# The first mixer's first 1024 columns, multiplied in step with the modulation

## The chip, the cores and the metric

The kernel runs on one core of a Trainium2 chip. The metric is the device time of one execution in microseconds (us), with the weights and inputs in HBM. The core's engines are TensorE (PE, its weight loads PEld), VectorE (DVE), ScalarE (ACT), GpSimd (POOL) and SyncE (SP), which issues nearly all loads.

## The reference

256 tokens of 1024 channels pass through three blocks, in float32. Only the start matters here:

```python
cond = silu(c)
mod = cond @ ada_w[layer] + ada_b[layer]          # 6 x 1024 values for each of 2 layers
shift1, scale1, gate1, shift2, scale2, gate2 = split(mod, 6)
hn = rmsnorm(x, norm1_w) * (1 + scale1) + shift1
# first mixer (mLSTM)
proj = hn @ w_in                                  # 3088 columns
qk = silu(causal_conv(proj[:, :1024], conv_w, conv_b))   # q: 512, k: 512
v, o, gates = proj[:, 1024:2048], proj[:, 2048:3072], proj[:, 3072:]
x = x + gate1 * (mixer(q, k, v, gates, o) @ w_out)
hn = rmsnorm(x, norm2_w) * (1 + scale2) + shift2
x = x + gate2 * swiglu(hn)
```

A second layer (a gated linear recurrence and a mixture of 8 experts) and a block with three kinds of attention and a feed-forward follow. They are the same in both kernels.

## The kernel before, in words

The activations lie transposed: 8 chunks of 128 channels on the partitions, 256 tokens along the free dimension. A weight matrix is read in tiles of 1 MiB, [128, 4, 512] (512 rows of 512 columns), by a generator, `all_weights`, that names them in the order of use. `weights()` hands out the next tile and prepares those after it, two ahead (`depth`). Most tiles are split by ScalarE and VectorE into a high and a low part in a shorter format (`whi`, `wlo`), and each product is then three products; tiles whose number stands in `WHOLE` are multiplied unsplit in float32, where each product shows as two records in the trace.

A load goes into a buffer `raw` (4 slots) or `raw2` (2 slots) and is issued on SP's queue when a slot is free. The first three tiles, columns 0 to 511 and half of 512 to 1023, are whole.

The modulation is done on VectorE. `ada_tile` (L478 to L492) loads 256 columns of `ada_w`, 1 MiB, and multiplies each of two blocks of 128 columns with `cond`, adding up along the row. There are 48 such tiles, 24 for each layer, numbered from 0 here. Tiles 0 to 3 give shift1 and 4 to 7 scale1; 8 to 11 give gate1, 12 to 15 shift2, 16 to 19 scale2. After the first norm a tile is done now and then between products: `ada_step(f)` adds up fractions and does one tile for each whole one. In the mixer that is one tile for each tile of weights (`between=step`), in the output's product 0.7 for each of the two tiles that have a `between`. `ada_until(20)` (in `run`) does what is left up to tile 19 before the next norm. These tiles take the `raw2` slots.

Before the first norm, x is squared by chunk on ScalarE. GpSimd adds up the squares of the first six chunks (`together=6`), TensorE then sums them and the last two over the partitions, a chain of small steps on VectorE makes r = 1 / root mean square from it, and TensorE spreads r over the partitions.

`first_norm` does tiles 0, 4, 1, 5, 2, 6, 3, 7 of the modulation; after each pair two chunks of the gain are known. From the second pair on it scales the chunks (VectorE) and adds the shift (ScalarE, into `full`, named `so` in the trace); at the end it splits `full` into act_hi and act_lo. Then `mlstm` multiplies: `convolved(0, q)` the first 512 columns, the two gates' rows (`small`), the chain for the decays, `convolved(1, k)` the next 512 columns with a modulation tile for each of its two weight tiles, then v (`proj_tok`) and the rest. A product of 512 columns holds two of the four accumulator banks `acc`.

The order on each engine is not the program's: a planner goes through the program with its own costs and gives each engine the instruction that comes first in the program among those that it takes for ready; a load is ready when its slot is free. The engines then run their lists in order. `behind(ins)` puts instructions after `ins` on the same engine. `hold` is a list of such instructions for the splits and modulation tiles to come. After the output's product it is set for two of them:

```python
self.hold = [[self.last_resid]] * 2
self.ada_until(20)
```

so the next two modulation tiles come after the last residual on VectorE. The norm that follows needs all of tiles 16 to 19, since `gain(0, 4, ...)` is one instruction over its 8 columns.

## Time and profile before

| what | value |
|---|---|
| time, median of 3 runs | 1485.22 us (1483.94 to 1486.9) |
| profiled execution, first to last instruction (span) | 1481.2 us |
| TensorE busy | 96% of the span, mean granted clock 0.977 |
| VectorE busy | 76% |
| ScalarE busy | 57% |
| transfers | 231 GB/s read over the span |

The profile gives the profiled execution's time as its span; the runs' time holds start and end as well. Busy times are sums of an engine's instructions; on TensorE products overlap, so its busy time is not work at its peak. In the timeline a row is a start, a duration, an engine, a line of the kernel, an operation, output <- inputs, and in brackets the idle time before it and what ended it. A line can be that of a helper: L165 is every product, L175 every step of ScalarE, L178 and L181 most of VectorE, L485 the modulation's products, L194 and L481 the loads of weights and of modulation.

### The profile page before, as it was taken

The numbers are of one execution on the slowest core, as the hardware profiler recorded it, in microseconds if no ns is written. First come the engines' busy times: TensorE is split into PE (matmuls) and PEld (weight loads), VectorE is DVE, ScalarE is ACT, GpSimd is POOL, SyncE is SP. The second block draws the span as 40 slices with busy tenths as digits, with TensorE's granted clock in tenths as the row PEclk, the third lists the DMA queues.
The fourth block names the chain that finished last, engine by engine and source line by source line (L and its number), as shares of the span: only waits on it lengthen the run. The fifth ranks groups of instructions, "written<-read, shape, count | busy, mean of one in ns | idle before, by whom it ended". The sixth has DMA issues, their size and how long they took to land.

```text
span 1481.2 us, 23294 instructions
## 1 busy us (share of the span) xinstructions
PE 1429.3 (96%) x9380; PEld 1292.7 (87%) x9380; DVE 1123.6 (76%) x1738; ACT 838.1 (57%) x1195; POOL 32.9 (2%) x36
## 2 busy tenths in 40 slices
PE   5999899999999998999999999999999999999998
PEld 4789899999999987888888888888878779999998
DVE  6887798887697786897898888888666566765554
ACT  2644444434775655777777777766545355544432
POOL 1000100001000020000000000000000000100000
PEclk7999999999899998999999999999999999999999
DMA  8975599989453334798998998995435234555542
GB/s 335 339 260 195 178 348 353 343 314 337 150 151 109 115 114 145 252 375 309 320 362 305 345 339 303 355 322 192 143 114 169 88 114 143 164 179 191 179 143 86
DMA packets 149508, 343.51 MB, mean 232 GB/s; under 512 B 5904, under 2 KB 27280, under 8 KB 149136
## 3 DMA queue, kind: packets, MB, share of 16 engines
q1 hardware_dynamic: 148240, 341.00, 66.1%
q8 instruction: 76, 1.25, 0.4%
q10 hardware_dynamic: 1152, 0.94, 0.2%
q14 instruction: 40, 0.33, 0.1%
HBM read 340.86 MB, written 1.05 MB: 231 GB/s over the span
## 4 chain that ended last, share of the span: by engine, by line
PE 58%; ACT 1%; DVE 1%; issue 0%; ACTq 0%
PE acc L165 38%; PE ps L165 18%; PE ps L1203 1%; ACT whi L175 1%; PE ps L1290 1%; PE ps L698 0%; DVE wlo L181 0%; ACT L175 0%; PE ps L1413 0%; DVE yel L178 0%; ACT yeh L175 0%; ACT e L175 0%; ACT sg L175 0%; DVE ss L677 0%; DVE e L185 0%
## 5 line engine op out<-in xcount | busy, mean ns | idle before, releaser
L181 DVE TENSOR_TENSOR wlo<-raw,whi 128x1024 fp32r<-128x1024 f32 (+2 forms) x564 | 646.9, 1182 | 148.2 <-ACT whi L175 147.6
L175 ACT ACTIVATE whi<-raw 128x1024 fp32r<-128x1024 f32 (+2 forms) x564 | 547.8, 1016 | 314.1 <-PE acc L165 164.3
L165 PE MATMUL acc<-act_hi,whi 128*128 128x256 f32 x1344 | 382.0, 285 | 2.6 <-ACT act_hi L175 2.4
L165 PE MATMUL acc<-act_lo,whi 128*128 128x256 f32 x1344 | 381.1, 284 | 0.0
L165 PE MATMUL acc<-act_hi,wlo 128*128 128x256 f32 x1344 | 379.6, 283 | 1.3 <-DVE wlo L181 1.3
L165 PEld LDWEIGHTS acc<-act_hi,whi 128*128 128x128 f32 x1344 | 255.2, 190 | 4.7 <-ACT act_hi L175 3.0
L165 PEld LDWEIGHTS acc<-act_hi,wlo 128*128 128x128 f32 x1344 | 255.5, 190 | 1.8 <-DVE wlo L181 1.5
L165 PEld LDWEIGHTS acc<-act_lo,whi 128*128 128x128 f32 x1344 | 255.8, 190 | 0.7
L165 PE MATMUL acc<-whi,act_hi 128*128 128x512 f32 (+1 forms) x560 | 217.5, 388 | 0.1
L165 PE MATMUL acc<-wlo,act_hi 128*128 128x512 f32 (+1 forms) x560 | 216.7, 387 | 0.0
L165 PE MATMUL acc<-whi,act_lo 128*128 128x512 f32 (+1 forms) x560 | 215.6, 385 | 0.0
L165 PEld LDWEIGHTS acc<-whi,act_hi 128*128 128x128 f32 x560 | 105.9, 189 | 20.3 <-issue 0.9
L165 PEld LDWEIGHTS acc<-wlo,act_hi 128*128 128x128 f32 x560 | 105.8, 189 | 20.2 <-issue 1.2
L165 PEld LDWEIGHTS acc<-whi,act_lo 128*128 128x128 f32 x560 | 105.7, 189 | 18.8 <-issue 0.3
L485 DVE SCALAR_TENSOR_TENSOR raw<-raw,cond 128x1024 f32<-128x1024 f32 x96 | 115.3, 1228 | 6.5 <-DMA raw<-in_ada_w_dram 6.5
L165 PE MATMUL ps<-hh,whi 128*128 128x256 f32 x352 | 99.6, 283 | 1.5 <-DVE x L178 1.5
L165 PE MATMUL ps<-hl,whi 128*128 128x256 f32 x352 | 99.5, 283 | 0.0
L165 PE MATMUL ps<-hh,wlo 128*128 128x256 f32 x352 | 99.4, 283 | 0.0
L165 PE MATMUL ps<-wlo,hth 128*128 128x512 f32 x176 | 69.0, 392 | 0.0
L165 PEld LDWEIGHTS ps<-hh,whi 128*128 128x128 f32 x352 | 67.4, 192 | 1.7 <-DVE x L178 1.7
L165 PE MATMUL ps<-whi,htl 128*128 128x512 f32 x176 | 68.8, 391 | 0.0
L165 PE MATMUL ps<-whi,hth 128*128 128x512 f32 x176 | 67.6, 393 | 0.0
(348 smaller groups left out, 1798.2 us busy)
## 6 DMA issues: line engine op xcount, KB each, us to landing
raw<-in_ada_w_dram SPq DMA_DIRECT2D x48, 1024.0 KB, 6.2
raw<-in_moe_w_down_dram SPq DMA_DIRECT2D x40, 1024.0 KB, 6.0
raw<-in_moe_w_up_dram SPq DMA_DIRECT2D x32, 1024.0 KB, 7.3
raw<-in_moe_w_gate_dram SPq DMA_DIRECT2D x32, 1024.0 KB, 7.1
raw<-in_w_in_dram SPq DMA_DIRECT2D x26, 1024.0 KB, 5.2
raw<-in_h_w_in_dram SPq DMA_DIRECT2D x16, 1024.0 KB, 5.8
raw<-in_m_w_in_dram SPq DMA_DIRECT2D x12, 1024.0 KB, 7.3
raw<-in_moe_w_gate_dram SPq DMA_DIRECT2D x16, 768.0 KB, 5.5
```

Source lines behind the costliest of these rows:

```text
L165: self.nc.tensor.matmul(out, l, r, start=start, stop=True, skip_group_check=True)
L175: return self.nc.scalar.activation(out, in_, f, **k)
L181: return self.nc.vector.tensor_tensor(out, a, b, op=op)
L485: last = self.nc.vector.scalar_tensor_tensor(w[:, i, :], in0=w[:, i, :], scalar=1.0, in1=self.cond, op0=ALU.mult, op1=ALU.mult, accum_out= ...
L1203: nc.tensor.transpose(hps[:, f * P : (f + 1) * P], h[:, f * P : (f + 1) * P], self.cst("ident"))
L1290: nc.tensor.transpose(pt[:, j * P : (j + 1) * P], e[:, j * P : (j + 1) * P], self.cst("ident"))
```

## The change

The four first weight tiles are cut the other way, 256 rows (two chunks) by 1024 columns, and all four are whole (`WHOLE` gets 3). `first_norm` does a round for each pair of modulation tiles: both tiles, the load of the weight tile that belongs to these two chunks (into `raw2`), gain, scale and shift of the two chunks, their split, and their products with all 1024 columns, into all four `acc` banks. `mlstm` gets these banks and convolves q and k from them, one after the other and before the gates' rows; the two modulation tiles that were done between k's products are no longer there. All modulation tiles of the first norm use `raw`. x is loaded in two halves, named before `conditions`, and its squares are no longer added up by GpSimd (`together=1`): TensorE sums each chunk. The chain of r is no longer put behind the modulation's products. Docstrings are taken out, which is left out here.

```diff
-WHOLE = {0, 1, 2, 12}
+WHOLE = {0, 1, 2, 3, 12}
...
-        yield from columns("m_w_in", *range(0, 3072, 512))
+        wv = a["m_w_in"].rearrange("(k p) n -> p k n", p=P)
+        yield from [wv[:, k : k + 2, 0:D] for k in range(0, DC, 2)]
+        yield from columns("m_w_in", *range(D, 3072, 512))
...
     def first_norm(self, x):
         act = self.act_tiles()
         g = self.t(self.cp, [P, 8], "gain01")
         shift = self.mod_part(0, 0)
+        banks = [self.bank("acc").rearrange("p (a s) -> p a s", a=2) for _ in range(4)]
         r = None
-
-        def normed(chunks):
-            for c in chunks:
+        for j in range(4):
+            self.ada_tile(0, j, "raw")
+            self.ada_tile(0, 4 + j, "raw")
+            self.tiles += 1
+            self.loaded.append(self.raw(next(self.plan), "raw2"))
+            sl = slice(2 * j, 2 * j + 2)
+            self.stt(g[:, sl], self.mod_part(0, 1)[:, sl], 1.0, self.vec("n1", 2 * j, 2), ALU.add, ALU.mult)
+            if j == 0:
+                r = self.stat_end()
+            for c in range(2 * j, 2 * j + 2):
                 t = self.t(self.tp, [P, S], "sq", 4)
                 self.stt(t, x[:, c, :], g[:, c : c + 1], r, ALU.mult, ALU.mult)
                 self.act(self.full[:, c, :], t, AF.Identity, bias=shift[:, c : c + 1])
-
-        for j in range(4):
-            self.ada_tile(0, j, "raw2" if j % 2 else "raw")
-            last = self.ada_tile(0, 4 + j, "raw")
-            sl = slice(2 * j, 2 * j + 2)
-            self.stt(g[:, sl], self.mod_part(0, 1)[:, sl], 1.0, self.vec("n1", 2 * j, 2), ALU.add, ALU.mult)
-            if j == 0:
-                with self.behind(last):
-                    r = self.stat_end()
-            if j == 1:
-                self.load()
-                normed(range(4))
-            if j > 1:
-                normed(range(2 * j, 2 * j + 2))
-        with self.behind(last):
-            for c in range(0, DC, 2):
-                last = self.split(*[t[:, c : c + 2, :] for t in act], self.full[:, c : c + 2, :])
+            last = self.split(*[t[:, sl, :] for t in act], self.full[:, sl, :])
+            (w,) = self.weights(False)
+            order = [(k, cb) for k in range(2) for cb in range(DC)]
+            if j == 3:
+                order.sort(key=lambda x: x[1])
+            for k, cb in order:
+                self.mm(banks[cb // 2][:, cb % 2, :], w[:, k, cb * P : (cb + 1) * P], self.full[:, 2 * j + k, :], j + k == 0 and cb % 2 == 0)
         self.last_normed = [i.ins for i in last]
+        self.prepare(self.depth)
         self.ada_owed, self.ada_now = 0.0, 8
-        return act
+        return act, banks
...
         with tc.tile_pool(name="cond", bufs=1) as pool:
+            for c in range(0, DC, 4):
+                nc.sync.dma_start(x[:, c : c + 4, :], a["xT"].rearrange("p (c s) -> p c s", c=DC)[:, c : c + 4, :])
             self.conditions(pool)
-            nc.sync.dma_start(x, a["xT"].rearrange("p (c s) -> p c s", c=DC))
-            self.stat_begin()
+            self.stat_begin(together=1)
...
-                act = self.first_norm(x)
-                act = self.mlstm(mlstm, act)
+                act = self.mlstm(mlstm, *self.first_norm(x))
...
-    def mlstm(self, pool, act):
+    def mlstm(self, pool, act, banks):
...
-            for b, bank in enumerate(self.proj_t(act, between=step if g else None)):
+            for b, bank in enumerate(banks[2 * g : 2 * g + 2]):
...
         convolved(0, q)
+        convolved(1, k)
         gp = self.bank()
...
-        convolved(1, k)
         for g in range(2):
```

## Rows read from the trace of the kernel before

**Rows 1.** The page, part 1: busy us, share of the span, instructions of TensorE.
```profile
PE 1429.3 (96%) x9380; PEld 1292.7 (87%) x9380; DVE 1123.6 (76%) x1738; ACT 838.1 (57%) x1195; POOL 32.9 (2%) x36
```

**Rows 2.** Windows: stretch, length, busy us per engine, granted clock, DMA share, GB/s.
```profile
20.00:24.00 4.00, 1.22 (x4) 0.93 (x4) 3.97 (x12) 0.00 (x0) 0.00 (x0) 0.50 1.02 408
...
28.00:32.00 4.00, 4.00 (x13) 3.21 (x13) 3.78 (x10) 0.00 (x0) 0.00 (x0) 0.65 0.99 355
32.00:36.00 4.00, 4.00 (x20) 3.02 (x19) 3.96 (x8) 1.54 (x3) 0.00 (x0) 1.00 0.32 122
72.00:78.40 6.40, 6.40 (x15) 4.31 (x15) 5.12 (x12) 4.46 (x8) 0.00 (x0) 0.50 0.38 119
```

**Rows 3.** Timeline of PE, first 61 us: start us, duration us, operation, count, idle before.
```profile
3.90 3.48 PE L165 MATMUL ps<-cst_base,vecs 128*128 128x128 f32 x16 [3.90 <-DMA cst_base<-in_cst_base_dram]
15.42 2.72 PE L165 MATMUL ps<-cst_base,sq 128*128 128x1 f32 x12 [8.04 <-POOL sq L410]
22.21 1.22 PE L165 MATMUL ps<-cst_base,st1y 128*128 128x128 f32 x4 [4.07 <-DVE st1y L178]
25.44 9.82 PE L165 MATMUL acc<-so,raw 128*128 128x256 f32 x32 [2.00 <-ACT so L175]
35.19 2.78 PE L165 MATMUL ps<-so,gate_w 128*40 128x256 f32 x12
...
40.21 6.31 PE L165 MATMUL acc<-so,raw 128*128 128x256 f32 x28 [1.18 <-ACT so L175]
46.45 1.06 PE L165 MATMUL ps<-so,gate_w 128*40 128x256 f32 x4
47.44 7.17 PE L165 MATMUL acc<-so,raw 128*128 128x256 f32 x32
54.26 0.47 PE L165 MATMUL acc<-act_hi,whi 128*128 128x256 f32 x1
...
60.08 0.40 PE L165 MATMUL acc<-whi,act_hi 128*128 128x512 f32 x1
```

**Rows 4.** Timeline of DVE, first 42 us.
```profile
10.16 1.23 DVE L485 SCALAR_TENSOR_TENSOR raw<-raw,cond 128x1024 f32<-128x1024 f32 x1 [5.98 <-DMA raw<-in_ada_w_dram]
...
18.18 0.16 DVE L187 TENSOR_SCALAR st1v<-ps 128x2 f32<-128x2 f32 x1 [1.72 <-PE ps L165]
...
19.24 1.22 DVE L485 SCALAR_TENSOR_TENSOR raw<-raw,cond 128x1024 f32<-128x1024 f32 x1
...
24.36 0.48 DVE L178 SCALAR_TENSOR_TENSOR sq<-x,gain,ps 128x256 f32<-128x256 f32 x1
...
39.14 0.86 DVE L178 SCALAR_TENSOR_TENSOR sq<-x,gain,ps 128x256 f32<-128x256 f32 x2
```

**Rows 5.** Lines of DVE, 40 to 60 us: count, busy us, mean ns, idle before.
```profile
L178 DVE SCALAR_TENSOR_TENSOR conv<-acc,vecs,conv 128x253 f32<-128x253 f32 (+2 forms) x12 | 5.3, 474 | 1.9 <-ACT conv L175 1.8
```

**Rows 6.** Timeline of all engines, end of the first mixer, 166 to 174 us.
```profile
166.34 0.86 DVE L178 SCALAR_TENSOR_TENSOR x<-acc,mod,x 128x256 f32<-128x256 f32 x2
...
167.12 1.21 DVE L485 SCALAR_TENSOR_TENSOR raw<-raw,cond 128x1024 f32<-128x1024 f32 x1
...
167.37 1.05 PE L165 MATMUL ps<-cst_base,sq 128*128 128x1 f32 x8 [1.10 <-ACT sq L175]
...
169.41 0.14 DVE L187 TENSOR_SCALAR st1v<-ps 128x2 f32<-128x2 f32 x1
169.51 0.37 SPq L481 DMA_DIRECT2D raw<-in_ada_w_dram  x1
...
169.71 0.17 DVE L178 SCALAR_TENSOR_TENSOR gain<-mod,vecs 128x8 f32<-128x8 f32 x1
...
171.17 0.16 DVE L178 SCALAR_TENSOR_TENSOR st1y<-st1h,st1y 128x2 f32<-128x2 f32 x1
...
172.73 1.26 DVE L178 SCALAR_TENSOR_TENSOR sq<-x,gain,ps 128x256 f32<-128x256 f32 x3 [1.40 <-PE ps L165]
```

**Rows 7.** DMA issues in 169 to 170 us: KB, us from issue to landing.
```profile
raw<-in_ada_w_dram SPq DMA_DIRECT2D x1, 1024.0 KB, 5.0
```

## The prediction

> **What bounds the kernel now.** I read the page's busy shares first. TensorE is busy for 96% of the span [rows 1], so what matters is what moves the start of its work, or opens a hole in it. Next came the windows of the first 100 us and then the timeline of each engine there, since the change is a change of the first mixer's start, and last the seam where its output meets the next norm.
>
> In the timeline TensorE's first large product starts at 25.44, and from 40.21 on it has no gap until the v products start at 60.08 [rows 3]. It runs on from there (busy for all of 6.40 us in the window at 72 us [rows 2], even at half clock), so whatever moves 60.08 moves what follows. What sets 25.44 is the factor r of the norm: its sums wait for GpSimd until 15.42 [rows 3], VectorE's chain for it runs from 18.18 with modulation products between its steps, and the first scaled chunk starts at 24.36 [rows 4], 1.08 us before the product. Transfers run at 408 GB/s meanwhile [rows 2], which is 2.6 us for a tile of 1.05 MB.
>
> The seam is the other place. After the last residual (166.34 + 0.86) VectorE does one modulation tile from 167.12 on, because `hold` puts it behind that residual; gain waits for it at 169.71, the chain of r ends at 171.33, and the next norm starts at 172.73 [rows 6]. TensorE has only small products there. So a microsecond added at this seam is a microsecond of the end.
>
> **The change part by part.** The modulation's tiles are numbered from 0.
>
> *When r is ready.* The six squares that GpSimd added up now go to TensorE one chunk at a time: 8 chunks, 32 records instead of 12. They cost 1.05/8 = 0.13 us each at full clock [rows 6] and 2.72/12 = 0.227 at half [rows 3], so 4.2 to 7.3 us, from the end of the spread of c (3.90 + 3.48 = 7.4) to between 11.6 and 14.7. The chain of r takes 171.33 - 169.41 = 1.9 us when nothing is put between its steps [rows 6], its spread 1.22 [rows 3]. The modulation tile 0 lands as before at 10.16 [rows 4] (x was ahead of it and still is), tile 4 2.6 us later; two products of 1.23 each bring VectorE to 15.2, and the small additions of tile 4 to about 15.5. Lower bound: r is done by then and the first product starts 1.08 later, at 16.6. Upper bound: the products of tile 1 stand inside the chain, as at 19.24 [rows 4]. Tile 1 now lands behind a weight tile, at 12.7 + 2 x 2.6 = 17.9, and from 17.9 the rest of the chain as before (19.24 to 25.44) gives 24.1. If VectorE runs the chain after tile 4 and before tile 1, it is 15.2 + 1.9 + 1.2 + 1.1 = 19.4. I take 19.5, because the gap between 15.2 and 17.9 in which tile 1 is not there is as long as the chain: 25.44 - 19.5 = **5.9 us earlier**, with 1.3 and 8.8 as ends.
>
> *TensorE's work from there to the v products.* Before, it is 60.08 - 25.44 = 34.6 us. Now there are four whole tiles of 32 records and 16 records for the gates: 9.82 for the first, which begins at half clock in either kernel (0.50 at 20 to 24 us, the 1.2 GHz level, after small products; 0.65 at 28 to 32, then 1.00 [rows 2]), 3 x 7.17, and 2.78 + 1.06 [rows 3], together 35.2. The whole fourth tile costs 7.17 where the split one took 60.08 - 54.26 = 5.8, and the wait of 1.18 before 40.21 goes. So **0.5 us later**. If the 32 sums keep the clock at full until the first tile, some of its records save half: 9.82 against 7.17 for a tile at full clock, 2.65 us; in the trace the clock is at half after 12 such sums, so I take none of it.
>
> *New waits.* The weights' tiles now take the two `raw2` slots, so the third's load waits until TensorE is through with the first, and the fourth's with the second. Landing goes in steps of 2.6 us from 10.16 on: tiles 0 and 4, a weight tile, 1, 5, a weight tile, 2, 6. Then 3 and 7, whose slots are free by 23, land at 30.8 and 33.4. The third weight tile, asked for at 19.5 + 9.8 = 29.3, comes behind them at 36.0; TensorE wants it at 36.5. A tile of v ahead of it makes it 2.1 late, two 4.7. The fourth, asked for at 36.5, lands 5.0 us later on idle queues [rows 7], 41.5, and is wanted at 43.7: one tile ahead costs 0.4, two 3.0. SP's queue is in order, so behind such a waiting load stand the modulation's last tiles and v's, and VectorE and ScalarE's splits wait for those. I take **0.5 us**, with 0 and 7.7 as ends. The modulation is not late: even behind the third weight tile, 7 lands at 36, and its norm (2.4 + 1.4 us of VectorE and ScalarE) is done by 40. The window at 32 us shows transfers at 0.32 now [rows 2], so there is room for the weights that come sooner.
>
> *Convolutions.* All four accumulators are held by the first product, so v's first two wait for the convolutions of four column blocks: 12 steps of VectorE at 0.474 [rows 5], 5.7 us. They start 1.8 us into the last tile, which is sorted by columns, and end at 43.7 + 1.8 + 5.7 = 51.2, before TensorE has done the last tile and the gates' products (54.7). Hidden; were the gates' products done earlier, v would start up to 3.8 us sooner, not later. The 7.2 us of VectorE's work that leave this stretch (a split of 2.4 and two modulation tiles of 2.4 each) are worth nothing there, since TensorE has the shorter end.
>
> First mixer: -5.9 + 0.5 + 0.5 = **-4.9 us**.
>
> *The seam.* The k columns' product was also the place where two modulation tiles were done (`between=step`, one for each tile of weights). Now 8 + 4 + 4 + 1 = 17 tiles are done when `ada_until(20)` comes, not 19. Three are left: 17, 18, 19. The first two are held behind the last residual; the third takes the slot of the first. It can be asked for only when VectorE is through with tile 17, at 169.5, where the trace issues the next tile now [rows 6], and lands 5.0 us later [rows 7], at 174.5. Its products take 2 x 1.2, additions and gain 0.5: 177.4, where the norm starts at 172.73 now [rows 6]. Tile 18 (2.4 us) and the chain of r (1.9 us, and 1.4 to its spread's end) fit in between, 169.5 to 175.2. That is **+4.7 us**, with 4.2 (a load half a microsecond quicker) and 8 (the chain put behind tile 19) as ends.
>
> By the Trainium skill, page "DMA: Bandwidth & Descriptors", section "Anatomy of one DMA", a transfer costs about 2.0 us and its bytes at 436 GB/s, here an estimate of 4.4 us, on another path than SP's; the row has 5.0. By the rule the seam would cost 4.1 and the sum would be 0.6 us lower; I stay with the row. The same page's "Rules for kernel authors" say to issue a transfer early and wait late, and tile 19 is issued after the point that it holds up: that speaks against this change, and the 5.0 us stand for it.
>
> Sum: -4.9 + 4.7 = **-0.2 us**. The profiled span is 1481.2, the median of the runs 1485.22; the 4.0 us around the span belong to start and end and stay. Forecast: 1485.0.
>
> **Rivals.**
> (a) *Faster.* The sums run at full clock and r is there when tile 4 is: the first product starts at 16.6 to 17.5, 8 to 8.8 us earlier, and the clock may save 2.6. Against it: the sums must run in half the time that the row at half clock has, and the third tile of weights then waits for its load (wanted at 33.6, landing 34 to 36), which takes back up to 2. -8 + 0.5 + 1 + 4.7 = -1.8 without the clock, -4.4 with it: 1481 to 1483. A stretch at clock 0.50 around 72 to 78 us [rows 2], after the many products of 8 rows, makes 6.4 us of what takes 3.2 at full; it may go with the new order, which would give about as much.
> (b) *Slower: the loads behind TensorE.* SP's queue puts the tiles of v or the modulation ahead of the third and fourth weight tile. It decides from two tiles ahead on: 4.7 for the third, 5 us with what the fourth adds, in place of my 0.5: -5.9 + 0.5 + 5 + 4.7 = +4.3, 1489.5. For it speaks that v's loads need only free slots; against it that they come later in the program.
> (c) *Slower: r behind tile 19 at the seam.* If VectorE's order puts the chain of r behind tile 19's products, its 1.9 and the spread's 1.4 come on top: +3.1, 1488.3. It decides where the plan takes the load for quicker than tile 18 and the chain, 4.3 us; now the chain stands behind the one held tile [rows 6].
> (d) *It doesn't do what it says.* The chain of r takes tile 1 and tile 5 into it as now, the first product starts at 24.1 and the stages follow the modulation no closer: -1.3 + 1.0 + 4.7 = +4.4, 1489.6.
>
> **How the numbers follow.** The forecast's case gets 0.50; (a) 0.25, (b) 0.10, (c) 0.07, (d) 0.08. A difference under 0.2%, 3.0 us, can't be told from none here. Of the forecast's case 0.40 lies within that, 0.07 below and 0.03 above; of (a) 0.15 lies below (the part with the clock) and 0.10 within; of (b), (c) and (d) 0.24 lie above and 0.01 within. That makes 0.22 faster, 0.51 the same, 0.27 slower. The range runs from 1479.8 (most of (a)) to 1490.5 (most of (b) to (d)); the likeliest case's own is 1482 to 1488.
>
> **What would show it.** Right: the first large product at 18 to 21 us; no wait over 1 us before the four tiles' products; v's products from 54 to 56; at the seam an issue of a modulation tile right after the first of two held ones, VectorE waiting some 2 us for it, and 4 to 5 us more between the last residual and the norm. Wrong: v's products before 52 or after 59, TensorE waiting for `raw`, tile 19 loaded before the last residual, or a seam no longer than before, which would make the change faster by 5 us.

## The result, and the profile after

The changed kernel takes 1493.61 us (median of 6 runs) where the kernel before takes 1484.58 beside it: 0.56% slower, ratio 1.0056, 95% interval [1.0037, 1.0074]. A second set of 6 runs gave 1490.56 against 1484.72, 1.0046 [1.0030, 1.0062]. So it costs 6 to 9 us; 1485.0 was forecast, and both medians lie above the range. The profiled execution is the fastest of its set (1486.21, span 1484.4). Its busy shares say nothing, as [rows 1] didn't:

```profile
PE 1432.0 (96%) x9384; PEld 1295.1 (87%) x9384; DVE 1120.3 (75%) x1736; ACT 832.6 (56%) x1191; POOL 26.9 (2%) x31
```

The timeline of TensorE in the first 58 us answers [rows 3] (start, duration, operation, count, idle before; in this kernel the modulation's products are at L487 and its loads at L483):

```profile
8.78 4.39 PE L165 MATMUL ps<-cst_base,sq 128*128 128x1 f32 x32 [0.99 <-ACT sq L175]
17.37 1.22 PE L165 MATMUL ps<-cst_base,st1y 128*128 128x128 f32 x4 [4.20 <-DVE st1y L178]
19.78 9.89 PE L165 MATMUL acc<-so,raw 128*128 128x256 f32 x32 [1.19 <-ACT so L175]
29.59 1.06 PE L165 MATMUL ps<-so,gate_w 128*40 128x256 f32 x4
30.58 7.17 PE L165 MATMUL acc<-so,raw 128*128 128x256 f32 x32
...
46.77 7.17 PE L165 MATMUL acc<-so,raw 128*128 128x256 f32 x32
53.87 1.06 PE L165 MATMUL ps<-so,gate_w 128*40 128x256 f32 x4
57.89 0.48 PE L165 MATMUL acc<-whi,act_hi 128*128 128x512 f32 x1 [2.96 <-DVE conv L178]
```

The first product comes at 19.78, 5.7 earlier than in [rows 3], and the tiles follow one another without a wait. But v starts at 57.89, only 2.2 earlier: TensorE waits 2.96 us for VectorE's convolution. VectorE there (beside [rows 5]):

```profile
44.87 0.69 DVE L181 TENSOR_TENSOR act_lo<-so,act_hi 128x512 fp32r<-128x512 f32 x1 [1.24 <-ACT act_hi L175]
49.83 1.00 DVE L178 SCALAR_TENSOR_TENSOR conv<-acc,vecs,conv 128x253 f32<-128x253 f32 x2 [4.27 <-ACT conv L175]
50.77 2.36 DVE L181 TENSOR_TENSOR wlo<-raw,whi 128x1024 fp32r<-128x1024 f32 x2
53.05 0.48 DVE L178 SCALAR_TENSOR_TENSOR conv<-acc,vecs,conv 128x255 f32<-128x255 f32 x1
53.44 2.35 DVE L181 TENSOR_TENSOR wlo<-raw,whi 128x1024 fp32r<-128x1024 f32 x2
55.71 2.42 DVE L178 SCALAR_TENSOR_TENSOR conv<-acc,vecs,conv 128x253 f32<-128x253 f32 x6
```

It idles 4.27 us, and then the splits of v's first two tiles, 4.7 us, stand between the steps of the convolution that frees v's banks; v starts behind the eighth of the nine steps shown, when the first bank is free. ScalarE's half of these splits stands between its own parts of the convolution:

```profile
49.70 3.88 ACT L175 ACTIVATE whi<-raw 128x1024 fp32r<-128x1024 f32 x4
...
53.94 1.00 ACT L175 ACTIVATE conv<-acc,vecs 128x256 f32<-128x256 f32 x2
```

The splits are late because SP asks for v's tiles behind the fourth tile, whose slot is free only at 37.8 (SP's queue; the last of these rows is the fourth tile and three of v):

```profile
29.70 0.37 SPq L194 DMA_DIRECT2D raw<-in_m_w_in_dram  x1
30.16 1.03 SPq L483 DMA_DIRECT2D raw<-in_ada_w_dram  x2
37.79 2.47 SPq L194 DMA_DIRECT2D raw<-in_m_w_in_dram  x4
```

The seam, all engines, beside [rows 6]:

```profile
164.32 0.86 DVE L178 SCALAR_TENSOR_TENSOR x<-acc,mod,x 128x256 f32<-128x256 f32 x2
...
165.11 1.21 DVE L487 SCALAR_TENSOR_TENSOR raw<-raw,cond 128x1024 f32<-128x1024 f32 x1
...
167.50 7.85 SPq L483 DMA_DIRECT2D raw<-in_ada_w_dram  x3
...
169.75 0.15 DVE L187 TENSOR_SCALAR st1v<-ps 128x2 f32<-128x2 f32 x1
...
172.57 1.23 DVE L487 SCALAR_TENSOR_TENSOR raw<-raw,cond 128x1024 f32<-128x1024 f32 x1 [0.89 <-DMA raw<-in_ada_w_dram]
...
175.18 0.17 DVE L178 SCALAR_TENSOR_TENSOR gain<-mod,vecs 128x8 f32<-128x8 f32 x1
```

VectorE does tile 17, tile 18 and the chain of r, waits 0.89 for tile 19, and comes to gain at 175.18 (before 169.71) and to the norm at 175.49 (before 172.73): 4.8 us longer from the last residual.

### Taking the half clock out

Two executions of one program differ by stretches in which TensorE is at a granted clock of 0.50, the 1.2 GHz level. Windows of the two profiles of the kernel before, the first and then the second, which has it for longer:

```profile
72.00:76.00 4.00, 4.00 (x9) 2.49 (x9) 2.72 (x6) 2.79 (x7) 0.00 (x0) 0.50 0.33 121
76.00:80.00 4.00, 4.00 (x13) 3.15 (x13) 4.00 (x9) 1.67 (x2) 0.00 (x0) 0.67 0.70 232
```
```profile
68.00:72.00 4.00, 4.00 (x8) 1.95 (x7) 2.24 (x8) 3.94 (x7) 0.00 (x0) 0.50 1.05 395
72.00:76.00 4.00, 4.00 (x8) 1.78 (x7) 1.31 (x4) 1.04 (x2) 0.00 (x0) 0.50 0.37 135
76.00:80.00 4.00, 4.00 (x9) 2.59 (x9) 2.87 (x7) 2.67 (x5) 0.00 (x0) 0.50 0.00 0
80.00:84.00 4.00, 4.00 (x15) 2.96 (x14) 4.00 (x10) 1.64 (x3) 0.00 (x0) 0.81 0.79 261
```

To compare, I sum busy PE time times (1 - clock) over windows of 4 us from 36 to 160 us and subtract it (at 0.50, half of a window's busy time is taken off). In the table, "first product" and "v" are the starts of the first large product and of the first v product on TensorE, "last residual" is the start of its last instruction, and the seam runs from there to the first instruction of the next norm. (The expectations of a5, b2 and c3 count the seam from the start of the last pair of residuals, 0.4 more; those of a2 and a3 from that pair's end, 0.5 less.) "Half" is the sum, and the ratio is to runs of the kernel before on the same chip. All times in us.

| kernel | first product | v | last residual | half | without half | seam | ratio [95%] |
|---|---|---|---|---|---|---|---|
| before | 25.4 | 60.1 | 166.7 | 3.4 | **163.3** | 6.0 | |
| a5 before again | 25.6 | 60.4 | 170.0 | 6.8 | **163.1** | 6.0 | |
| changed | 19.8 | 57.9 | 164.7 | 1.7 | **163.0** | 10.8 | 1.0056 [1.0037, 1.0074] |
| a1 changed again | 19.8 | 57.8 | 167.8 | 4.9 | **162.8** | 10.6 | 1.0046 [1.0030, 1.0062] |
| a2 tiles into v | 20.3 | 58.2 | 172.9 | 6.0 | 166.9 | 6.1 | 1.0042 [1.0028, 1.0056] |
| a3 before, 3 at seam | 25.7 | 60.4 | 165.7 | 1.7 | 164.0 | 10.8 | 1.0043 [1.0026, 1.0059] |
| a4 v's loads first | 22.3 | 62.9 | 169.5 | 3.2 | 166.4 | 10.7 | 1.0044 [1.0026, 1.0061] |
| c1 convolution whole | 19.7 | 56.7 | 163.3 | 0.0 | 163.3 | 10.8 | 1.0035 [1.0019, 1.0050] |
| b2 tiles into output | 22.3 | 59.3 | 174.0 | 6.8 | 167.2 | 6.1 | 1.0050 [1.0034, 1.0066] |
| c3 c1 and b2 | 22.4 | 59.1 | 170.6 | 3.4 | 167.2 | 6.1 | 1.0025 [1.0011, 1.0040] |
| d1 tiles into the gap | 19.6 | 66.9 | 173.6 | 6.9 | 166.8 | 6.0 | 1.0055 [1.0034, 1.0077] |
| d2 c1 and d1 | 20.1 | 62.8 | 174.0 | 8.1 | 166.0 | 6.1 | 1.0026 [1.0012, 1.0040] |
| d3 tile 19 early | 22.4 | 59.7 | 169.5 | 5.1 | 164.4 | 10.8 | 1.0054 [1.0038, 1.0070] |
| e1 changed less 2 tiles | 19.6 | 57.8 | 164.9 | 1.7 | 163.1 | 6.1 | 1.0003 [0.9989, 1.0018] |
| e2 before less 2 tiles | 25.5 | 60.2 | 166.9 | 3.4 | 163.5 | 6.0 | 0.9995 [0.9980, 1.0010] |
| e3 before, sums alone | 22.5 | 57.2 | 162.2 | 1.7 | **160.4** | 6.0 | 0.9984 [0.9969, 0.9999] |
| e4 c1 less 11 tiles | 22.2 | 58.7 | 169.1 | 6.8 | 162.3 | 6.1 | 1.0004 [0.9988, 1.0020] |
| f1 e3 again | 22.4 | 57.2 | 162.1 | 1.7 | **160.4** | 6.0 | 0.9974 [0.9961, 0.9986] |
| f2 sums and pairs | 20.1 | 62.3 | 167.3 | 4.6 | 162.7 | 6.0 | 1.0012 [0.9997, 1.0026] |

Without the half clock the two profiles of before agree to 0.2 us, those of the changed kernel too, and between the kernels the last residual differs by 0.3 us. The first mixer's gain is gone; the seam's 4.7 is there.

### The profile page after: what moved, and what is told of

Its sections match the earlier page's. It is cut to its first block, busy times and chain, and to the rows that moved or that the text cites. A ratio compares the mean times of both kernels' runs of the same rounds, so it can differ in the third digit from the quotient of the medians.

```text
span 1484.4 us, 23298 instructions
## 1 busy us (share of the span) xinstructions
PE 1432.0 (96%) x9384; PEld 1295.1 (87%) x9384; DVE 1120.3 (75%) x1736; ACT 832.6 (56%) x1191; POOL 26.9 (2%) x31
## 3 DMA queue, kind: packets, MB, share of 16 engines
HBM read 340.86 MB, written 1.05 MB: 230 GB/s over the span
## 4 chain that ended last, share of the span: by engine, by line
PE 58%; ACT 1%; DVE 1%; issue 0%; ACTq 0%
PE acc L165 38%; PE ps L165 18%; PE ps L1205 1%; ACT whi L175 1%; PE ps L1292 1%; PE ps L700 0%; DVE wlo L181 0%; ACT L175 0%; PE ps L1415 0%; DVE yel L178 0%; ACT yeh L175 0%; ACT e L175 0%; ACT sg L175 0%; DVE ss L679 0%; DVE e L185 0%
## 5 line engine op out<-in xcount | busy, mean ns | idle before, releaser
L165 PE MATMUL acc<-act_hi,whi 128*128 128x256 f32 x1328 | 378.2, 286 | 5.0 <-ACT act_hi L175 4.7
L487 DVE SCALAR_TENSOR_TENSOR raw<-raw,cond 128x1024 f32<-128x1024 f32 x96 | 114.3, 1219 | 7.0 <-ACT sq L175 6.1
```

The lines of the kernel that those rows point to most:

```text
L165: self.nc.tensor.matmul(out, l, r, start=start, stop=True, skip_group_check=True)
L487: last = self.nc.vector.scalar_tensor_tensor(w[:, i, :], in0=w[:, i, :], scalar=1.0, in1=self.cond, op0=ALU.mult, op1=ALU.mult, accum_out= ...
```

## The experiments

In the expectations T (later T2, T3) is the account held at that point and R (R1, R2) its rival; a run is then said to bear out one of them, or neither.

**a1, a5: each kernel once more.**

> The changed kernel once more, unaltered, for a second profile. Its first profiled execution has a span only 3.2 us over the one of before, its other executions some 8 to 9. T (the seam's 4.7 us are the loss, the front gives 2.2 back, the rest is small and spread): a profile with a span of 1484 to 1488, the v products again at 57.9, the seam again 4.8 longer. R1 (there is a further loss of 4 to 5 us that the first profile happened not to have): a span of 1489 to 1493, and a stretch in which the two profiles of one program drift apart by that much; if the v products start at 60 or later it sits in the front (a load that lands late), if only the stretch from the third tile of weights on moves, in the loads; if it lies behind 1000 us, in the experts.

> The kernel before once more, unaltered, for a second profile: what two executions of one program differ by. T (the stretches of TensorE at half clock come and go from one execution to the next, 1.6 to 3.4 us each): the same start of the v products at 60.1 and the same seam of 6.4 us, and differences of 1 to 4 us only where a stretch at half clock is there in one and not in the other. R (they are fixed by the program): the two profiles agree to 0.5 us everywhere.

The spans were 1488.5 and 1486.7, against 1484.4 and 1481.2. The starts of v are the same to 0.4 us. The repeat of the changed kernel is longer at half clock, first right after the idle 2.96 us before v (windows of the first profile, then of the repeat):

```profile
59.00:63.00 4.00, 4.00 (x19) 3.23 (x18) 3.97 (x9) 1.60 (x6) 0.00 (x0) 1.00 1.05 395
```
```profile
59.00:63.00 4.00, 4.00 (x13) 3.10 (x12) 3.97 (x9) 1.60 (x6) 0.00 (x0) 0.57 1.04 395
```

13 records where there were 19. The span of a1 lies between T's and R1's; what drifts apart is the time at half clock, as a5's T has it, and no load.

**a3: the seam's change alone, on the kernel before.**

```diff
-            for b, bank in enumerate(self.proj_t(act, between=step if g else None)):
+            for b, bank in enumerate(self.proj_t(act)):
```

> The kernel before, with one edit: the k columns' product does no modulation tiles, so three are left for the seam, as in the changed kernel; the front is otherwise as before. T: the seam from the last residual to the next norm grows from 5.5 to 10.3 us and the time by 4 to 5 us, to 1488.5 to 1490; the v products start up to 1 us earlier, as VectorE has 4.8 us less to do there, so the whole may be 3.5 to 5. R1 (the loss is in the front, in the order of the loads): within 1.5 us of the kernel before. R2 (the change's whole loss of 8 to 9 us comes from leaving three tiles): 8 us slower, 1492 or more.

1490.47, 1.0043: as much as the changed kernel (1.0046, on the same chip), and the seam is 10.8. The time is a little above T's range, and v isn't earlier (60.4), though VectorE has less to do there. So the two tiles that leave the k columns' product are enough for the whole of the loss.

**e1, e2: the same two tiles left out, of the changed kernel and of the one before.** Tiles 18 and 19, or 8 and 9, get the bias alone:

```diff
+        if layer == 0 and j in (18, 19):
+            o = 2 * j
+            with self.held():
+                return self.nc.vector.tensor_copy(self.mod[:, o : o + 2], self.vec("ada_b", o, 2)).ins
```

> The changed kernel without the products and loads of modulation tiles 18 and 19 (their columns get the bias alone): one tile is left at the seam, as in the kernel before. What is left of the change is the front. As I predicted it (front -4.9): 1480 to 1481 against 1485 of the kernel before. T2 (the front gives nothing that lasts): seam 6.0, the last residual at 163 with the half clock taken out, the time 4 to 5.5 us under the changed kernel's and within 1.5 us of the kernel before's, 1484.5 to 1487.

> The kernel before without the products and loads of modulation tiles 8 and 9, the two that stand in the k columns' product (their columns get the bias alone). T2 (they have a free place there): the v products and the last residual within 1 us, the time within 1.5 us of the kernel before's, 1483.5 to 1486. R (they are on the path there too, as anywhere): 3 to 5 us faster, 1480 to 1482, and then the changed kernel only moves what was paid already.

1.0003 and 0.9995: both T2. The two tiles cost nothing in the k columns' product and everything at the seam, and the rest of the change, all of its front, is worth nothing that can be measured (e1's interval runs from 1.6 us faster to 2.7 slower): not the 4.9 us that I forecast.

**d3: is it the late load?**

```diff
-                self.hold = [[self.last_resid]] * 2
-                self.ada_until(20)
+                self.hold = [[self.last_resid]] * 3
+                self.ada_until(19)
+                self.ada_tile(0, 19, "raw")
+                self.ada_now = 20
```

> The changed kernel, but the last of the three modulation tiles at the seam is loaded into a buffer of its own, so that its load doesn't wait for tile 17. As I predicted it, the seam's 4.7 us come from that late load: without it the seam would be 7 to 8.5 us (one more tile of 2.4 on the old 6.0) and the time 2.5 to 4 us below the changed kernel's. T2: the late load hides behind tile 18 and the chain of r, what costs is VectorE's time for two more tiles; the three tiles then run on end, 7.1 us, and the chain and its spread, 3.4, come behind them: a seam of 10.5 to 11.2 and the same time within 1.5 us.

1.0054, and VectorE at the seam:

```profile
169.12 0.86 DVE L178 SCALAR_TENSOR_TENSOR x<-acc,mod,x 128x256 f32<-128x256 f32 x2
...
175.77 1.21 DVE L487 SCALAR_TENSOR_TENSOR raw<-raw,cond 128x1024 f32<-128x1024 f32 x1
...
176.91 0.15 DVE L187 TENSOR_SCALAR st1v<-ps 128x2 f32<-128x2 f32 x1
...
180.29 1.26 DVE L178 SCALAR_TENSOR_TENSOR sq<-x,gain,ps 128x256 f32<-128x256 f32 x3 [1.46 <-PE ps L165]
```

No wait for a load is left, the chain of r now comes behind the third tile, and the seam is 10.8 all the same: T2. VectorE has 4.8 us more to do either way. In the changed kernel the load shows for 0.89, but the wait for the spread of r (1.40 in [rows 6], 1.46 here) is hidden in return, behind tile 19. Three tiles with the load in time and the chain of r ahead of the third could save at most that 0.89; this order wasn't run. My forecast had the seam's size right and its cause too narrow.

**a2, b2: the two tiles elsewhere.** `self.ada_step(f * 1.5)` in v's product (for `f * 1`), or in the output's (for `f * 0.7`).

> The changed kernel, but the v columns' product does 1.5 modulation tiles for each tile of weights instead of 1, so two more tiles are done there and one is left for the seam, as before the change. T (the seam loses 4.7 us because tile 19's load is asked for only after tile 17): the distance from the last residual to the next norm falls from 10.3 to 5.5 us, and the time by 4 to 5 us against the changed kernel, to 1487 to 1490 by its median; against the kernel before it is then between 2 us faster and 4 slower. R (the seam's wait is hidden by what comes later, or VectorE has no room for two more tiles in the v products): the seam is shorter but the time within 1.5 us of the changed kernel's, 1492 to 1495.

> The changed kernel, but the output product of the first mixer does 1.5 modulation tiles for each tile of weights in place of 0.7, so that three come there and one is left for the seam, as before the change. The run with 1.5 in the v products showed the seam back at 6.4 us and the 5 us lost again ahead of it, where VectorE sets the pace. T: in the output product VectorE waits for TensorE for some 3 us twice, so two more tiles of 2.4 us fit; the last residual moves by 0 to 2.4 us, the seam is 6.4 instead of 11.1, and the time falls by 2.5 to 4.7 us, to 1486 to 1489. R (VectorE has no room for them anywhere after the k columns' product has gone): the last residual moves by 4 us or more, the time within 1 us of the changed kernel's.

The seam is back at 6.1 in both, and both are as slow as the changed kernel: R and R. The last residual comes 4 us later, since TensorE now waits for VectorE's chains ahead of it (a2's longest wait, then b2's two; in b2 v starts 1.4 later too, with the slow sums described at the end):

```profile
142.02 5.18 PE L165 MATMUL ps<-cst_base,r8y 128*128 128x128 f32 x32 [3.25 <-DVE r8y L178]
```
```profile
143.43 3.81 PE L165 MATMUL ps<-cst_base,r8y 128*128 128x128 f32 x32 [2.28 <-DVE r8y L178]
148.88 7.17 PE L165 MATMUL acc<-num,raw 128*128 128x256 f32 x32 [1.64 <-DVE num L181]
```

In b2 the products of a modulation tile stand between the steps of that chain (138.65 and 139.88); the free place in the output's product, which T counted on, was used by only one tile more.

**a4, c1: v earlier.** In a4, v's first two tiles are asked for before the modulation's last pair; in c1 after that pair and before the fourth tile, and what follows the first four blocks' convolution on VectorE stays behind it (c1's edit; `last` is the convolution's last instruction):

```diff
-            self.loaded.append(self.raw(next(self.plan), "raw2"))
+            src = next(self.plan)
+            if j == 3:
+                early = [self.raw(next(self.plan)) for _ in range(2)]
+                self.tiles += 2
+            self.loaded.append(self.raw(src, "raw2"))
...
+        self.loaded.extend(early)
...
-        convolved(0, q)
+            return last.ins
+
+        hold = self.behind(convolved(0, q))
+        hold.__enter__()
...
+        hold.__exit__(None, None, None)
```

> The changed kernel, but the first two tiles of v's weights are asked for before the modulation's last pair (tiles 3 and 7) and the fourth tile of the first weights, not behind them. T (the v products start at 57.9 and not at 55 because their tiles land behind the fourth, so that VectorE's splits of them stand between the steps of the convolution that frees the banks): the splits are done before the last tile's products end, the convolution runs unbroken from 49.8, and the v products start at 55.5 to 56.5, 1.5 to 2.4 us earlier, if the modulation's tiles 3 and 7 don't become late; the time falls by as much, to 1490 to 1492. R1 (loads bind: the last pair or the fourth tile now lands behind v's tiles): TensorE waits before the fourth large tile and v starts at 58 or later, the time the same or up to 3 us longer. R2 (the banks are freed by ScalarE's part, not by VectorE's): the splits move and v stays at 57.9.

> The changed kernel with two edits at the start of the v products: v's first two tiles of weights are asked for after the modulation's last pair but before the fourth tile of the first weights, and what follows (the later tiles' splits, the gates, the modulation) stays behind the convolution of the first four column blocks. T (the 2.2 us instead of 4.9 at the v products come from splits that stand between the steps of the convolution, and the idle TensorE before it then falls to half clock): VectorE does the splits before 49.8 where it idles now, the convolution's 12 steps run in 5.3 to 6 us, the v products start at 55.2 to 56 instead of 57.8, TensorE idles under 1 us there and stays at full clock at 58 to 63; the time falls by 2 to 4 us against the changed kernel, to 1487 to 1489.5. R (ScalarE's part of the convolution or the landing of v's tiles binds as well): v at 57 or later, the time within 1 us of the changed kernel's.

a4 came out as its R1: VectorE split v's tiles ahead of modulation tiles 3 and 7, TensorE waited 3.0 us for the fourth product, and v started at 62.9. c1 has the convolution whole, and v at 56.7, where T has 55.2 to 56 and R 57 or later. VectorE, then ScalarE:

```profile
47.01 2.35 DVE L181 TENSOR_TENSOR wlo<-raw,whi 128x1024 fp32r<-128x1024 f32 x2
51.95 1.52 DVE L178 SCALAR_TENSOR_TENSOR conv<-acc,vecs,conv 128x253 f32<-128x253 f32 x3 [2.58 <-ACT conv L175]
54.46 2.50 DVE L178 SCALAR_TENSOR_TENSOR conv<-acc,vecs,conv 128x253 f32<-128x253 f32 x6 [1.00 <-ACT conv L175]
```

```profile
51.36 0.55 ACT L175 ACTIVATE conv<-acc,vecs 128x256 f32<-128x256 f32 x1
...
53.88 1.00 ACT L175 ACTIVATE conv<-acc,vecs 128x256 f32<-128x256 f32 x2
```

Without VectorE's splits in the way TensorE still waits 1.82 of the 2.96 us. The rest is ScalarE's: its first part of the convolution comes at 51.36 (49.23 in the changed kernel), behind a split of a further tile whose load landed only at 50.40 and which the edit doesn't hold back, and its next parts come at 53.88, no earlier than in the changed kernel. The time, 1489.00, is in T's range, but its interval overlaps those of the changed kernel. And the last residual stays at 163.3: TensorE waits later instead (its only waits between v and the output's product):

```profile
132.77 3.81 PE L165 MATMUL ps<-cst_base,r8y 128*128 128x128 f32 x32 [0.99 <-DVE r8y L178]
138.03 3.29 PE L165 MATMUL acc<-num,raw 128*128 128x256 f32 x14 [1.45 <-DVE num L181]
```

No half clock was left from 36 to 160 us in that profile.

**c3: c1 and b2 together.**

> Both of these together: v's first two tiles before the fourth tile with the convolution unbroken, and three modulation tiles in the output product. T: the two gains add, 2 to 4 and 2.5 to 4.7 us: 1482.5 to 1486.5, that is at the kernel before's time or up to 3 us faster, and the last residual to the next norm in 6.4 us. R: what one gains the other takes (VectorE is the bound from the v products to the output product): within 1.5 us of the better of the two alone, and slower than the kernel before.

1.0025, and a median of 1489.41 beside c1's 1489.00: R.

**d1, d2: the two tiles in VectorE's gap before 49.8.** Without and with c1's edits:

```diff
             self.ada_tile(0, 4 + j, "raw")
+            if j == 3:
+                self.ada_tile(0, 8, "raw")
+                self.ada_tile(0, 9, "raw")
...
-        self.ada_owed, self.ada_now = 0.0, 8
+        self.ada_owed, self.ada_now = 0.0, 10
```

> The changed kernel, but the modulation's tiles 8 and 9 are asked for before the fourth tile of the first weights, so that VectorE can do them where it idles now, from 45.6 to 49.8; 19 tiles are done when the seam comes, as before the change. What the runs so far say (T2): with the time at half clock taken out of the profiles, the last residual comes at 163 us in the kernel before, in the changed one and in the one with the earlier v; the seam's 4.7 are 2 tiles of 2.4 us of VectorE that had a free place beside the k columns' product, and there is none from the v products to the seam (two tiles there cost 5). The gap before 49.8 is the free place that is left: the seam is 6.0 again, the last residual at 163 to 164.5 with the half clock taken out, the time 3 to 4.7 us below the changed kernel's, 1486 to 1488.5. R (the loss is the order in which the loads are asked for): v's tiles land 5 us later still, v starts at 60 or later, and the time stays within 1.5 us of the changed kernel's.

> The same two modulation tiles in the gap, on top of the version in which v's first two tiles are asked for before the fourth and the convolution of the first four blocks is unbroken. T2: VectorE now has 4.9 us of modulation and 4.7 of splits for a gap of 4.2, so the convolution begins up to 5 us later and v starts at 58 to 61 instead of 56.7; the seam is 6.0; the last residual, which did not follow v's start in the run without these tiles, at 163 to 166 with the half clock taken out; 1485 to 1489. R (the order of the loads is what costs): v at 56 to 57 and the time 4 us or more below the version without the two tiles, 1482 to 1485.

Both missed T2 at v. In d1 the tiles fitted into the gap, but the gates' chain and the splits then came ahead of the convolution, and v started at 66.9. In d2 the four loads ahead of the fourth weight tile filled the slots, its load was late, and TensorE waited:

```profile
53.00 10.16 PE L165 MATMUL acc<-so,raw 128*128 128x256 f32 x32 [5.30 <-DMA raw<-in_m_w_in_dram]
```

d1's start of v and its time are as R has them, and its loads are late too (SP takes 8.36 us for the four issues that took 2.47). So neither run tells T2 from R: here the loads and VectorE's order did bind, and whether the gap alone would have paid isn't settled.

**e4: c1 with VectorE relieved.** Eleven modulation tiles (8 to 16, 18, 19) left out, as in e1.

> The version with the earlier v products (56.7), without the products and loads of modulation tiles 8 to 16, 18 and 19 (their columns get the bias alone): VectorE has 21 us less to do between the v products and the last residual. T2 (VectorE takes the gain back in that stretch: TensorE waited 1.0 and 1.5 us for it at 131.8 and 136.6): these waits go, and the last residual comes 2 to 3.5 us earlier than without this edit, at 160 to 161.5 with the half clock taken out; 1482 to 1484. R (TensorE's own work sets the last residual): it stays at 163 with the half clock taken out, only the seam is 6.0 instead of 10.8: 1484 to 1486.

1.0004. In the profile the waits at 132 and 138 are down to 0.16 and none, and v to the last residual takes 103.6 without the half clock (c1 106.5, the kernel before 103.2): of those 2.9 us some 2 are TensorE's waits and 1 is its busy time. That is T2's mechanism. But the last residual, 162.3, missed T2's 160 to 161.5 (in this execution the sums were slow, the first product came at 22.2 and v 1.9 later than in c1), and the median, 1485.98, is in R's range and no better than e1's ratio. So the 2.9 us are read from one profile; the times don't show them.

**e3, f1: the sums alone, on the kernel before.**

```diff
-            nc.sync.dma_start(x, a["xT"].rearrange("p (c s) -> p c s", c=DC))
-            self.stat_begin()
+            self.stat_begin(together=1)
```

with x in two halves ahead of `conditions`, as in the change.

> The kernel before with only the sums of the change: x comes in two halves ahead of the spread of c, and TensorE sums the squares of one chunk at a time, without GpSimd. The chunks of the first product are still scaled after tiles 1 and 5 of the modulation. T: r is done by 17 to 20, the first product starts at 23 to 25 (bound by tiles 1 and 5 now), at most 2 us earlier, and the time is within 1.5 us of the kernel before's. R (r alone set 25.4): the first product at 20 to 21, and the time up to 4 us lower.

> The kernel before with only the sums of the change, once more. In its first profile the first product is at 22.45, the v products at 57.2, 2.9 earlier than before, and the last residual at 160.4 with the half clock taken out, 2.8 earlier. T3 (in the kernel before TensorE has no wait from the first product to the last residual, so an earlier start comes through): the same three times within 0.5 us, and 1.5 to 3.5 us under the kernel before. R (the first run was a lucky draw): within 1 us of the kernel before's time.

0.9984 and 0.9974 (1481.74 against 1485.67): faster than both kernels, 2.4 to 3.9 us. e3's first product, at 22.5, lies between T's and R's, its time is R's; f1 is T3, with 3.9 us a little more than its 3.5. TensorE in f1:

```profile
8.70 4.23 PE L165 MATMUL ps<-cst_base,sq 128*128 128x1 f32 x32 [0.99 <-ACT sq L175]
19.18 1.22 PE L165 MATMUL ps<-cst_base,st1y 128*128 128x128 f32 x4 [6.25 <-DVE st1y L178]
22.41 8.64 PE L165 MATMUL acc<-so,raw 128*128 128x256 f32 x32 [2.00 <-ACT so L175]
...
57.20 0.40 PE L165 MATMUL acc<-whi,act_hi 128*128 128x512 f32 x1
```

The first product is 3.0 earlier, v 2.9, the last residual 2.8 without the half clock. In the old order the start comes through to the last residual.

**f2: and the pairs.** The chunks are scaled in pairs with their modulation tiles, the column tiles as before:

```diff
-            if j == 1:
+            if j == 0:
                 self.load()
-                normed(range(4))
-            if j > 1:
-                normed(range(2 * j, 2 * j + 2))
+            normed(range(2 * j, 2 * j + 2))
```

> The same, and the chunks are scaled two at a time with their modulation tiles, with the first tile of weights asked for before tiles 1 and 5; the products stay in tiles of 512 rows by 512 columns. T3: the first product at 19.5 to 20 as in the changed kernel, but half of its records wait for tiles 1 and 5, at 24.5 to 25.5; the v products 0 to 1.5 us earlier than with the sums alone, at 55.7 to 57.2, and the time 2 to 4.5 us under the kernel before. R (VectorE's two tiles at a time and the later loads take it back): v at 57.5 or later, the time no better than with the sums alone.

R, and worse: the first product is at 20.1, and then TensorE waits 0.79 and 3.17 us for chunks that VectorE scales behind their modulation tiles (it has no gap from 19.1 to 39.7 and scales the last pair at 38.87, where it did so at 39.14 before), and 1.23 for the second weight tile, which is asked for behind six modulation tiles. v is at 62.3, the time as before.

## Why the prediction was wrong, step by step

- *When r is ready* (the start of the first product): forecast 19.5, bounds 16.6 and 24.1; 19.78. Right. The sums took 4.39, near the lower bound, and tile 4's products stood inside the chain instead of ahead of it.
- *TensorE's work to the v products*: forecast 35.2; 54.93 - 19.78 = 35.15. Right.
- *New waits on the slots*: forecast 0.5; none before the four tiles. The price of SP's order showed elsewhere, in v's late tiles. That is rival (b)'s mechanism with another place and 3 us in place of 5.
- *Convolutions hidden, end at 51.2*: the first step that failed. The step that v waited for, only the eighth, ended at 57.7. I counted 12 steps of 0.474 from 45.5 and left out that VectorE and ScalarE run their lists in order, with 4.7 and 3.9 us of splits in them that the kernel before did while TensorE was still at the k columns. The first step came at 49.83 and not at 45.5, in part because three of the gates' four products stand ahead of the last tile and not behind it. In c1, with no split between VectorE's steps, v starts 4.8 after the first step (51.95 to 56.72); from 49.83 that would be 54.6, an estimate, before TensorE is through at 54.93. The wait is 2.96 us; with it the gain at v is 2.2 instead of 4.9.
- *"Whatever moves 60.08 moves what follows"*: the second. From v to the last residual the kernel before takes 106.65 - 3.44 = 103.2 without the half clock, the changed kernel 106.83 - 1.72 = 105.1. The window of that stretch and TensorE's waits in it, before and then changed:

```profile
60.08:166.73 106.65, 106.01 (x666) 91.92 (x664) 79.57 (x146) 49.82 (x77) 6.09 (x5) 0.97 0.70 242
62.53 0.26 PE L837 MATMUL ps<-cst_base,u 8*128 8x8 f32 x2 [0.18 <-DVE u L178]
```
```profile
57.89:164.72 106.83, 105.13 (x664) 92.02 (x664) 80.19 (x150) 50.86 (x83) 6.14 (x5) 0.98 0.63 218
76.00 0.26 PE L840 MATMUL ps<-cst_base,u 8*128 8x8 f32 x2 [0.58 <-DVE u L178]
135.35 3.81 PE L165 MATMUL ps<-cst_base,r8y 128*128 128x128 f32 x32 [0.17 <-DVE r8y L178]
139.65 7.17 PE L165 MATMUL acc<-num,raw 128*128 128x256 f32 x32 [0.49 <-DVE num L181]
```

It waits 1.05 more, all of it for VectorE, and is busy for 0.8 more. A busy share of 6.40 in 6.40 [rows 2] shows that an engine has no gap now, not that its suppliers would be ready earlier. c1, with v another 1.2 earlier, gained nothing at the last residual. In e4's profile, with VectorE relieved, the waits and the extra busy time are both gone (busy 102.7 without the half clock, 102.6 before, 103.7 in c1): so it is VectorE that takes them, as far as one profile shows it. Why VectorE has less room than in the kernel before, with as many tiles there, I can only read from the trace: the gates' rows are complete at 54.9 instead of 47.5 [rows 3], and the transposes of u come at 76.0 where they came at 62.5. That wasn't tried by itself.

- *The other rivals*: (a) and (d) didn't come, the first product was on time. Of (a)'s two conditions the sums' held (0.137 us each), but r then waited for VectorE. Nor did (c) come, the chain of r stood ahead of tile 19.
- Together the first mixer: -2.2 at v, +1.05 and +0.8 behind it, -0.3 in place of **-4.9**. This is the term that was wrong.
- *The seam*: forecast +4.7; +4.8, and +4.8 in a3. Right in size. In the changed kernel the path is the one forecast, issue at 167.50, landing at 172.57, tile 19, norm, with a wait of 0.89 where I had some 2. But the late load alone isn't its price: d3, without that wait, has the same seam, so VectorE's time for two tiles is enough. By the Trainium skill (page "DMA: Bandwidth & Descriptors", section "Anatomy of one DMA") the load would have taken 4.4, an estimate from a fit for another path than SP's. It landed in 5.0, as the row before had it, so the trace doesn't agree; all but 0.89 of it was hidden.

The sum at equal clock: spans less the half clock after 36 us are 1460.8 and 1461.3 for before, 1466.4 and 1466.2 for the changed kernel: 5.2 slower, of which -0.3 first mixer, 4.7 seam, and 0.8 behind the norm. Those 0.8 are no more than two profiles of one program differ by there: e3 and f1, with the same last residual, have 1459.5 and 1458.0. What lifts the 5.2 to the measured 6 to 9 isn't shown. One candidate is the start: in 5 of 12 profiles of kernels with this front the sums take 7.0 us and not 4.4, the first product comes at 22.3, and v some 1.5 to 2.4 later than in a like kernel with quick sums. If that came as often in the changed kernel, whose own two profiles have quick sums, it would be 0.6 to 1.0 on average, an estimate. The rest of the spread is stretches at half clock, which both kernels have; whether the changed one has more of them is open.

## What to carry to other kernels

When a stage is rebuilt, list the work of the other engines that had its place beside the old one: here two tiles of modulation were free beside the k columns' product, cost their full 2.4 us each at the seam, and moved the last residual by 4 us in v's product and in the output's. A gain at the start of a stage counts only at its end: follow the next engine's list in its order up to there, and take out what the clock does before you compare two profiles. Of a change with several parts, try the cheapest alone: the early sums gave 0.2 to 0.3% that the rest of the change took back.

## What the runs showed that I had not expected

- Time lost at half clock between 36 and 160 us comes in steps: 0.0, 1.7, 3.4, 5.1 or 6.8, to 0.1, in 14 of the 19 profiles. One program had 3.4 in one execution and 6.8 in the next.
- In those 5 profiles with the slow sums, the 32 records take 0.22 us each and not 0.137, yet the granted clock's row shows 1.00 from 4 to 36 us. That row seems to lack an entry there, and the durations of equal records are the better witness.
